# Attention queries: turned once in the projection, stored turned, with the row of maxima placed by a transpose and eight small copies

## Chip, core and metric

The kernel runs on one core of a Trainium2 chip. The metric is the time of one execution in device microseconds (us), the median of several runs. TensorE (PE) multiplies matrices and transposes tiles, VectorE (DVE) and GpSimd (POOL) work on elements, ScalarE (ACT) evaluates functions and copies, SyncE (SP) issues most DMAs. SBUF is the working memory with 128 partitions; PSUM holds what TensorE writes, in eight banks of 128 x 512 float32.

## What is computed

One layer over 2048 latent tokens of width 1024, with 256 context tokens that only supply keys and values:

```python
p_x = modulate(x, norm1_g, sh1, sc1) @ w_in        # k | v | q | gMLP u | gMLP v | two gates
q_x = apply_rope(rmsnorm(q_heads(q_x), q_norm_g), cos, sin) * HEAD_DIM ** -0.5
k_x = apply_rope(rmsnorm(kv_heads(p_x[..., :K_W]), k_norm_g), cos, sin)
s = jnp.einsum('bkgqd,bknd->bkgqn', q, k, preferred_element_type=jnp.float32)
attn = softmax(s) @ v                              # 8 query heads of 64, 2 key heads
x = x + g1 * branch_merge(attn, gmlp, gate_a, gate_b, w_br_attn, w_br_gm, w_out)
x = x + g2 * (jnp.square(jax.nn.relu(modulate(x, norm2_g, sh2, sc2) @ w_ff1)) @ w_ff2)
```

All arrays are float32. The change concerns the queries `q` and the softmax of `s`.

## The kernel before, in words

The kernel has four stages, one after the other: projection (`project`, L994), attention (`attend`, L1109), the merge of the branches with the output projection (`merge`, L1240), and the feed-forward part (`ffn`, L1767). A float32 product is made of float32r products of a rounded "high" half and a remainder, the "low" half.

**Projection.** Tokens come in four blocks of 512 (`TB`), two of them at a time. `pairs_run` (L636) makes the columns up to the gates, `gates` (L965) the gate columns. Beside these products a list `work` of generators is stepped by `tick` (L680), a few operations at a time. One of them is `queries_work` (L755), once for each block of 512 tokens: it loads the raw queries (L760 to L762), normalises each head, rotates it (`rope`, L468; its last VectorE instruction is L483) and stores 128-token rows to the DRAM tensor `q_d[b]` of 512 tokens x 512 columns (L773), in two halves `c` of four heads. `keys_work` (L717) does likewise for the keys, but splits them into halves first (L738, L739), turns them on TensorE by `transposes` (L187; each transpose is at L189) and stores them turned. `mixing` (L802), the gMLP branch, turns its result in the same way (L845 to L855) and stores it by ScalarE's DMA queue (L857).

**Attention.** A unit (class `Unit`, L1989) is two heads of one block of 512 queries: 16 units, four for each block. `attend` goes through a unit's 18 key tiles of 128 keys in three thirds of six (`GROUP`), `gi` = 0, 1, 2. For each key tile, a score step, `first` (L2083) multiplies the keys (high and low halves stacked on 128 partitions) by the high half of the queries, `second` (L2094) adds the high keys times the low half of the queries, and ScalarE takes the exponential of the sum (L2111). The softmax maximum is subtracted inside `second`: partition 0 of the low-query operand holds minus the maximum, one number for each query, and partition 0 of the key operand `KB` holds 1 (the constant `lead`, L203, copied at L1803).

The next units are prepared inside the running one. In the code `nxt` is the unit one later, `far` the one two later, `old` and `older` the ones before. The maxima of `nxt` and `far` come from separate products with high halves alone (`maxima`, L2038: matmuls L2053, VectorE reductions L2059 and L2064). Then, after each third's score steps, come the products with the values of the third before (`values`, L2114; matmuls L2121, row sums on GpSimd L2137 and VectorE L2134), the sums of probabilities (`sums`, L2159), and `join` (L2147). The queries of a unit go this way:

- `load` (L1999), first third, for `far`: one DMA brings 512 tokens x 128 columns into `qt`; GpSimd zeroes a part of `pb` (L2010).
- `cast` (L2012), first third: ScalarE rounds `qt` to the high half, written twice, into `pa` (L2013). `remainder` (L2015), end of the first third: VectorE writes the low half into `pb` (L2016).
- `queries` (L2032), middle third, after the third key tile: eight transposes of `pa` on TensorE (L2026) and two evictions by ScalarE (L2028) give `qa`, the high operand of each head.
- `reference` (L2068), end of the middle third, for `nxt`: VectorE reduces the maxima (L2070) and writes minus the maximum into a column of `pb` (L2071).
- `low_queries` (L2076), after the last third's score steps, for `nxt`: eight transposes of `pb` and two evictions give `qb`, the low operand with the maxima in partition 0.

The first two units are prepared in the projection's closing gates by the function `tail` (L1812).

**What sets the order.** Tile tags name pools of buffers: `h` has 40 (keys, values, query operands), `t4` 8, `t2` 6 (`POOLS`, L55); PSUM has eight banks of tag `b` in attention, four `a` and four `b` in the projection. A scheduler orders the instructions; `order` (L1863) ties it. In attention TensorE and VectorE keep the order of the code, other engines do not; in the projection nearly nothing is fixed. The first writers of the buffers of one tag always keep the order of the code.

## Time and profile before

| what | us |
|---|---|
| median of 3 runs (3070.08 to 3071.9) | 3070.73 |
| the profiled execution's own time | 3072.42 |
| its span, first to last instruction | 3070.6 |
| projection, from the start | about 755 |
| attention, 16 units | 755 to 1436 |
| merge and feed-forward part | 1436 to the end |
| all transposes at L189: TensorE busy in 695 to 755 / 755 to 1436 | 4.25 / 30.02 |

The granted TensorE clock was 0.988 over the span. Views of the profile used below: the page's first part gives busy time by engine; the table of stretches gives busy time of each engine between two moments of the span, with the clock and the DMAs; the timeline lists instructions in order of time, alike ones merged into one line with their count (start, duration, engine, line of the kernel, operation, tiles written <- read, and in brackets the idle time before and what ended it); a line's own view gives shortest, median and longest duration in ns; the waits give who waited for whom, total us, times, and the longest. PEld is TensorE's loading of weights, which overlaps PE. A merged line's duration runs to the end of its last instruction, and TensorE's instructions overlap, so the spacing of starts says more than the durations.

### The profile page before, as it was taken

To read this page: it belongs to the slowest core of one execution; us is meant where nothing else is said; L and a number is where in the kernel's file an instruction comes from. 1 tells how busy PE (TensorE), PEld (TensorE's weight loads), DVE (VectorE), ACT (ScalarE), POOL (GpSimd) and SP (SyncE) were. 2 spreads that over 40 slices of the span, in tenths; PEclk is the share of its full clock that TensorE was granted. 3 is DMA by queue.
4 is the path that set the end of the run, shared out by engine and by line. 5 is a ranking of instruction groups with operands and counts; after the bars stand their busy time and mean duration, and the time that the engine had idled before them with its cause. 6 is when DMAs were issued, how large, how long until landed. Compare 5 with 4: busy or idle time off the path is not lost.

```text
span 3070.6 us, 38002 instructions
## 1 busy us (share of the span) xinstructions
PE 2981.3 (97%) x13501; PEld 2256.5 (73%) x13501; DVE 2070.4 (67%) x3006; ACT 1457.8 (47%) x2350; POOL 656.7 (21%) x488
## 2 busy tenths in 40 slices
PE   6999999989999999999999989999999999999999
PEld 4877788866555555555888878888777888888887
DVE  4876577875887677667655588776576666654555
ACT  5645765653555545545322254444454344444442
POOL 0000000001888888886222200000000000000000
PEclk9999999999999999999999999999999999999999
DMA  8686656644011000004676558888776544448554
GB/s 293 211 268 209 226 191 205 202 152 129 28 36 42 15 5 18 11 8 132 233 214 208 183 171 310 310 302 293 263 227 221 190 152 152 152 152 288 206 206 151
DMA packets 386591, 534.33 MB, mean 174 GB/s; under 512 B 32912, under 2 KB 204096, under 8 KB 386400
## 3 DMA queue, kind: packets, MB, share of 16 engines
q1 hardware_dynamic: 376624, 515.89, 50.4%
q10 hardware_dynamic: 9776, 16.01, 1.4%
q8 instruction: 106, 1.74, 0.2%
q14 instruction: 85, 0.70, 0.1%
HBM read 367.69 MB, written 164.10 MB: 173 GB/s over the span
## 4 chain that ended last, share of the span: by engine, by line
PE 84%; DVE 6%; DMA 5%; ACT 2%; issue 2%; SPq 0%; ACTq 0%; DVEq 0%
PE b L1546 13%; PE b L1545 13%; PE b L1547 13%; PE b L2121 8%; PE b L2088 5%; PE b L2107 4%; PE b L183 4%; PE b L185 4%; PE b L184 4%; PE b L2053 3%; PE a L1545 3%; PE a L1546 3%; PE a L1547 3%; PE b L189 2%; DMA f<-in_w_in 1%
## 5 line engine op out<-in xcount | busy, mean ns | idle before, releaser
L2064 DVE TENSOR_REDUCE ts<-b 128x1 f32<-128x512 f32 x512 | 314.7, 681 | 142.2 <-PE b L2053 142.2
L2137 POOL TENSOR_TENSOR ac<-ac,p 128x512 f32<-128x512 f32 x216 | 300.3, 1423 | 69.4 <-ACT p L2111 68.8
L1661 DVE TENSOR_TENSOR b<-b,b 128x1024 fp32r<-128x1024 f32 x170 | 200.7, 1220 | 128.9 <-ACT b L1660 127.6
L2111 ACT ACTIVATE p<-b 128x512 f32<-128x512 f32 x384 | 199.8, 615 | 167.4 <-PE b L2107 156.2
L1660 ACT CAST b<-b 128x1024 fp32r<-128x1024 f32 x170 | 170.7, 1051 | 225.1 <-PE b L1547 107.9
L1546 PE MATMUL b<-b,b 128*128 128x512 f32 x680 | 266.3, 392 | 5.6 <-DVE b L1661 5.6
L1545 PE MATMUL b<-b,b 128*128 128x512 f32 x680 | 267.1, 393 | 3.3 <-ACT b L1728 1.4
L1547 PE MATMUL b<-b,b 128*128 128x512 f32 x680 | 265.3, 390 | 0.0
L2137 POOL TENSOR_TENSOR ac<-ac,t 128x512 f32<-128x512 f32 x152 | 217.5, 1456 | 0.0
L2088 PE MATMUL b<-h,h 128*128 128x512 f32 x576 | 200.9, 419 | 3.1 <-ACT t L2169 1.7
L2107 PE MATMUL b<-h,h 128*128 128x512 f32 x576 | 180.6, 395 | 0.0
L2121 PE MATMUL b<-p,h 128*64 128x512 f32 x768 | 175.3, 598 | 0.0
L1546 PE MATMUL b<-hb,b 128*128 128x512 f32 x446 | 173.8, 390 | 0.0
L1555 DVE TENSOR_TENSOR f<-f,b 128x512 f32<-128x512 f32 x160 | 109.1, 682 | 82.1 <-issue 48.3
L1545 PE MATMUL b<-hb,b 128*128 128x512 f32 x415 | 161.8, 390 | 0.0
L1547 PE MATMUL b<-hb,b 128*128 128x512 f32 x415 | 161.3, 389 | 0.0
L2010 POOL MEMSET t<- 128x512 f32 x16 | 8.4, 525 | 700.2 <-DMA tb_d<-t 677.9
L1546 PEld LDWEIGHTS b<-b,b 128*128 128x128 f32 x680 | 128.1, 188 | 35.6 <-DVE b L1661 8.9
L1545 PEld LDWEIGHTS b<-b,b 128*128 128x128 f32 x680 | 128.0, 188 | 32.4 <-ACT b L1660 2.5
L2088 PEld LDWEIGHTS b<-h,h 128*128 128x128 f32 x576 | 106.9, 190 | 61.0 <-DVE ts L2064 19.4
L1547 PEld LDWEIGHTS b<-b,b 128*128 128x128 f32 x680 | 128.1, 188 | 26.4
L1558 ACT ACTIVATE f<-f 128x512 f32<-128x512 f32 x96 | 60.5, 630 | 148.8 <-DVE f L1555 148.8
(428 smaller groups left out, 7416.7 us busy)
## 6 DMA issues: line engine op xcount, KB each, us to landing
ao_d<-f SPq DMA_DIRECT2D x224, 256.0 KB
f<-in_w_ff SPq DMA_DIRECT2D x48, 1024.0 KB
b<-ao_d SPq DMA_DIRECT2D x85, 512.0 KB
b<-w2o_d SPq DMA_DIRECT2D x85, 512.0 KB
w2o_d<-f SPq DMA_DIRECT2D x112, 256.0 KB
f<-in_w_in SPq DMA_DIRECT2D x44, 512.0 KB
f<-x_d SPq DMA_DIRECT2D x64, 256.0 KB
hb<-ao_d SPq DMA_DIRECT2D x54, 256.0 KB
```

Of the source, the lines that this page charges most:

```text
L183: mm(ps, sh, mh, start=start, stop=False)
L1545: mm(ps, wh, hh, start=start and k == 0, stop=False, skip_group_check=True)
L1546: mm(ps, wh, hl, start=False, stop=False, skip_group_check=True)
L1547: mm(ps, wl, hh, start=False, stop=k == len(w) - 1, skip_group_check=True)
L1660: nc.scalar.copy(h, f32(l))
L1661: nc.vector.tensor_tensor(out=l, in0=f32(l), in1=f32(h), op=ALU.subtract)
L2064: nc.vector.tensor_reduce(out=self.mx[:, t, h, c : c + 1], in_=ps[h], axis=AX.X, op=ALU.max)
L2088: self.nc.tensor.matmul(self.pts[j][h], k.KA[c][self.kv][:, ks], self.qa[h], start=True, stop=False, skip_group_check=True,)
L2107: self.nc.tensor.matmul(s, k.KB[c][self.kv][:, ks], self.qb[h], start=False, stop=True, skip_group_check=True,)
L2111: self.nc.scalar.activation(pt[h], s, AF.Exp)
L2121: nc.tensor.matmul(self.o[h * HD : (h + 1) * HD, :], k.V[c][:, i, self.kv * HD : (self.kv + 1) * HD], pt[h], start=j == 0, stop=j == NKT - 1,)
L2137: nc.gpsimd.tensor_tensor(out=self.acc[e][:, h], in0=old[:, h], in1=pt[h], op=ALU.add)
```

## The change

`queries_work` turns the rotated queries on TensorE, evicts them by ScalarE and stores them from ScalarE's queue; `q_d[b]` becomes four tensors of 128 columns x 512 tokens, one for each pair of heads, i.e. one for each unit. A unit's `load` brings each head's 64 rows twice, into the upper and the lower 64 partitions (four DMAs of 64 rows). `cast` makes `qa` from that directly, `remainder` makes `qb`; `turned`, `queries` and `low_queries` go, with `pa`, `pb` and the memset. `cast` moves from the first third to the middle one, `remainder` to the end of the last. `reference` only reduces the maxima; `leading`, in the last third after key tile 16, the fifth of its six, transposes the 128 x 8 maxima into an 8 x 128 tile, ScalarE copies it to SBUF, and SyncE issues eight DMAs of 512 bytes each within SBUF that put the pieces into partition 0 of the two `qb`. The sign moves into `lead`, which becomes -1. In `qb`, partitions 1 to 63 now hold low halves; `KB` is zero there.

```diff
--- before.py
+++ after.py
@@ -200,7 +200,7 @@
         nc.vector.memset(self.ones, 1.0)
         self.lead = cp.tile([P, 1], F32, name="lead")
         nc.vector.memset(self.lead, 0.0)
-        nc.vector.memset(self.lead[0:1], 1.0)
+        nc.vector.memset(self.lead[0:1], -1.0)
         self.G1 = cp.tile([P, KC, 2], F32, name="G1")
         self.S1 = cp.tile([P, KC, 2], F32, name="S1")
         self.G2 = cp.tile([P, KC], F32, name="G2")
@@ -215,7 +215,10 @@
         def spill(n, shape):
             return [dp.tile(shape, F32, tag=f"{n}{b}", name=f"{n}_d{b}") for b in range(NB)]
 
-        self.q_d = spill("q", [TB, NH * HD])
+        self.q_d = [
+            [dp.tile([P, TB], F32, tag=f"q{b}_{p}", name=f"q_d{b}_{p}") for p in range(NH // 2)]
+            for b in range(NB)
+        ]
         self.gm_d = spill("gm", [512, TB])
         self.at_d = spill("at", [512, TB])
         self.ta_d = spill("ta", [D, TB])
@@ -770,11 +773,19 @@
             yield
             qo = self.m4([TT, 4, HD])
             self.rope(tabs, raw, qo, self.m4([TT, 4, HD]), 4)
-            nc.sync.dma_start(
-                self.rows(self.q_d[b], slice(c * 256, (c + 1) * 256)),
-                qo.rearrange("p t h d -> p t (h d)"),
-            )
-            yield
+            yield
+            for f in range(2):
+                ps = self.bank([TB])
+                self.transposes(
+                    ps,
+                    [
+                        qo[:, t, 2 * f : 2 * f + 2].rearrange("p h d -> p (h d)")
+                        for t in range(TT)
+                    ],
+                )
+                ot = self.t2([TB])
+                nc.scalar.copy(ot, ps)
+                nc.scalar.dma_start(self.q_d[b][2 * c + f], ot)
 
     def raw_values(self, b, j, c):
         x = self.m4([TT, 4, HD])
@@ -1119,22 +1130,19 @@
                 for j in group:
                     u.first(j)
                     u.second(j)
-                    if j % GROUP == 2 and far:
-                        if gi == 0:
-                            far.load()
-                        elif gi == 1:
-                            far.queries()
+                    if j % GROUP == 2 and far and gi == 0:
+                        far.load()
+                    if j % GROUP == 4 and nxt and gi == 2:
+                        nxt.leading()
                     if not nxt:
                         next(late, None)
                     elif i and j % GROUP == 4:
                         next(mod, None)
-                if gi == 2 and nxt:
-                    nxt.low_queries()
                 if step:
                     step.maxima(3)
                 for f in pend:
                     f()
-                if gi == 0 and far:
+                if gi == 1 and far:
                     far.cast()
                 if gi == 2 and old:
                     old.sums()
@@ -1143,8 +1151,8 @@
                 if gi == 0:
                     if older:
                         older.inverse()
-                    if far:
-                        far.remainder()
+                if gi == 2 and far:
+                    far.remainder()
                 if gi == 1:
                     if nxt:
                         nxt.reference()
@@ -1817,8 +1825,6 @@
                 key_load(0)
                 u.cast()
                 u.remainder()
-            elif (g, p) == (n, 1):
-                u.queries()
             elif (g, p) == (n + 1, 1):
                 low_load(0)
             elif (g, p) == (n, 5):
@@ -1829,8 +1835,6 @@
                     v.cast()
                     v.remainder()
                     value_load((0, 1))
-                if (g, p) == (n, 6):
-                    v.queries()
                 if (g, p) == (n + 1, 6):
                     key_load(1)
                     value_load((2, 3, 4))
@@ -1840,7 +1844,7 @@
                 if (g, p) == (n + 1, 3):
                     u.maxima(len(u.todo))
                     u.reference()
-                    u.low_queries()
+                    u.leading()
                     v.maxima(6)
 
         self.project(tail)
@@ -1998,42 +2002,22 @@
 
     def load(self):
         k, nc = self.k, self.nc
-        self.qt = k.t2([TT, 2, HD])
-        nc.sync.dma_start(
-            self.qt.rearrange("p t h d -> p t (h d)"),
-            k.q_d[self.b].rearrange("(t p) c -> p t c", p=P)[
-                :, :, self.p * P : (self.p + 1) * P
-            ],
-        )
-        self.pa = k.t4([TT, 2, 2, HD], F32R)
-        self.pb = k.t4([TT, 2, P])
-        nc.gpsimd.memset(self.pb[:, :, :, :HD], 0.0)
+        self.raw = [k.t2([TB]) for _ in range(2)]
+        for h, raw in enumerate(self.raw):
+            src = k.q_d[self.b][self.p][h * HD : (h + 1) * HD]
+            for i in range(2):
+                nc.sync.dma_start(raw[i * HD : (i + 1) * HD], src)
 
     def cast(self):
-        self.nc.scalar.copy(self.pa, self.qt.unsqueeze(3).broadcast_to([P, TT, 2, 2, HD]))
+        self.qa = [self.k.h2([TB], F32R) for _ in range(2)]
+        for q, raw in zip(self.qa, self.raw):
+            self.nc.scalar.copy(q, raw)
+        self.mx = self.k.small([TT, 2, NB + 1])
 
     def remainder(self):
-        self.nc.vector.tensor_tensor(
-            out=self.pb[:, :, :, HD:], in0=self.qt, in1=f32(self.pa[:, :, :, 0, :]),
-            op=ALU.subtract,
-        )
-
-    def turned(self, src):
-        k = self.k
-        out = []
-        for h in range(2):
-            ps = k.bank([TB])
-            k.transposes(ps, [src(t, h) for t in range(TT)])
-            q = k.h2([TB], F32R)
-            self.nc.scalar.copy(q, ps)
-            out.append(q)
-        return out
-
-    def queries(self):
-        self.qa = self.turned(
-            lambda t, h: f32(self.pa[:, t, h]).rearrange("p a d -> p (a d)")
-        )
-        self.mx = self.k.small([TT, 2, NB + 1])
+        self.qb = [self.k.h2([TB], F32R) for _ in range(2)]
+        for q, hi, raw in zip(self.qb, self.qa, self.raw):
+            self.nc.vector.tensor_tensor(out=q, in0=raw, in1=f32(hi), op=ALU.subtract)
 
     def maxima(self, n):
         k, nc = self.k, self.nc
@@ -2066,15 +2050,25 @@
                     )
 
     def reference(self):
-        nm = self.k.small([TT, 2])
-        self.nc.vector.tensor_reduce(out=nm, in_=self.mx, axis=AX.X, op=ALU.max)
-        self.nc.vector.tensor_scalar(
-            out=self.pb[:, :, :, 0:1], in0=nm.unsqueeze(3), scalar1=-1.0, scalar2=None,
-            op0=ALU.mult,
-        )
-
-    def low_queries(self):
-        self.qb = self.turned(lambda t, h: self.pb[:, t, h, :])
+        k, nc = self.k, self.nc
+        self.nm = k.small([2, TT])
+        nc.vector.tensor_reduce(
+            out=self.nm.rearrange("p h t -> p t h"), in_=self.mx, axis=AX.X, op=ALU.max
+        )
+
+    def leading(self):
+        k, nc = self.k, self.nc
+        n = 2 * TT
+        ps = k.bank([P])
+        nc.tensor.transpose(ps[:n], self.nm.rearrange("p h t -> p (h t)"), k.ident)
+        row = k.t2([P])
+        nc.scalar.copy(row[:n], ps[:n])
+        for h in range(2):
+            for t in range(TT):
+                nc.sync.dma_start(
+                    f32(self.qb[h])[0:1, t * P : (t + 1) * P],
+                    row[h * TT + t : h * TT + t + 1],
+                )
 
     def keys(self, j):
         c, i = (0, j) if j < CTX // P else ((j - 2) // TT + 1, (j - 2) % TT)
```

## The prediction, made before the result was known

> **What bounds the kernel now.** I read the page first, then the busy time by stretch of the span, then TensorE's timeline inside two attention units.
>
> ```profile
> PE 2981.3 (97%) x13501; PEld 2256.5 (73%) x13501; DVE 2070.4 (67%) x3006; ACT 1457.8 (47%) x2350; POOL 656.7 (21%) x488
> PE 84%; DVE 6%; DMA 5%; ACT 2%; issue 2%; SPq 0%; ACTq 0%; DVEq 0%
> ```
>
> TensorE is busy 97% of the span, and the chain that ended last runs through it for 84%. The next rows (stretch, its length, then busy us of PE, PEld, DVE, ACT, POOL, then clock, DMA share, GB/s) show two stretches of the projection and one attention unit.
>
> ```profile
> 100.00:400.00 300.00, 285.97 (x1359) 236.55 (x1358) 201.03 (x369) 173.62 (x270) 0.00 (x0) 0.99 0.70 230
> 400.00:695.00 295.00, 272.69 (x1281) 231.30 (x1280) 226.18 (x407) 165.71 (x263) 1.05 (x2) 0.96 0.59 185
> 1223.00:1266.00 43.00, 43.00 (x208) 23.73 (x206) 30.16 (x44) 22.23 (x43) 36.22 (x28) 1.00 0.04 13
> ```
>
> In attention TensorE never rests (43.00 of 43.00) at full clock, and no other engine is full. So there each TensorE instruction taken away shortens the unit by its pitch, unless it covered another engine's lag. In the projection TensorE idles 14.0 and 22.3 us: work put there is nearly all paid for. The transposes alone, by stretch:
>
> ```profile
> 695.00:755.00 60.00, 4.25 (x32) 3.60 (x30) 0.98 0.50 158
> 755.00:1436.00 681.00, 30.02 (x232) 27.03 (x232) 0.99 0.08 24
> ```
>
> All 232 of the attention stretch are queries being turned: 14 units x 8 for the high halves, 15 x 8 for the low halves with the maximum; in the closing gates (695 to 755) another 24 of the 32 are. Their 30 us of busy time overlap, so I price them by when the next instruction starts.
>
> **The change, part by part.** Units 13 and 14, TensorE alone. Unit 14 is the last but one: no unit follows its successor, so its middle third turns no queries and is otherwise the same. That is the change's first half, already in the trace.
>
> ```profile
> 1317.34 1.37 PE L2053 MATMUL b<-h,h 64*128 64x512 f32 x6
> 1318.64 3.65 PE L2121 MATMUL b<-p,h 128*64 128x512 f32 x16
> ...
> 1324.84 0.73 PE L2088 MATMUL b<-h,h 128*128 128x512 f32 x2
> ...
> 1331.40 1.03 PE L2053 MATMUL b<-h,h 64*128 64x512 f32 x6
> 1332.42 3.65 PE L2121 MATMUL b<-p,h 128*64 128x512 f32 x16
> ...
> 1338.62 0.89 PE L2088 MATMUL b<-h,h 128*128 128x512 f32 x2
> ...
> 1344.65 1.03 PE L189 MATMUL b<-ident,t 128*128 128x128 f32 x8
> 1345.61 1.39 PE L2053 MATMUL b<-h,h 64*128 64x256 f32 x10
> ...
> 1367.59 0.73 PE L2088 MATMUL b<-h,h 128*128 128x512 f32 x2
> ...
> 1380.40 0.88 PE L2088 MATMUL b<-h,h 128*128 128x512 f32 x2
> ```
>
> A. *High halves no longer turned.* The middle third takes 13.78 us in unit 13 (1324.84 to 1338.62) and 12.81 in unit 14 (1367.59 to 1380.40): 0.97 less. 14 units x 0.97 = **13.6 us**. By a pitch of 0.1 us per transpose alone it would be about 11; that is the lower end.
>
> B. *Low halves no longer turned; a transpose of the maxima five steps into the last third instead.* Eight transposes held TensorE 0.96 us (1344.65 to 1345.61).
>
> ```profile
> L189 PE MATMUL b<-ident,t x296: 270/272/328, 22.9 to 1387.2; 128*128 128x128 f32 x148
> L189 PEldq EVENT_SEMAPHORE  x61: 51/51/2516, 23.3 to 2306.2; - x61
> ```
>
> Against that stand four costs. (1) One new transpose, of 128x8: between 0.12 (0.96 / 8) and 0.27 (one instruction's busy time, nothing overlapped); I take 0.15, near the run of eight. (2) The transposes gave ScalarE time to free banks. At the first third's end, where nothing stands between scores and maxima, the six maxima matmuls take 1.30 us (1317.34 to 1318.64), in the middle third 1.02 (1331.40 to 1332.42): 0.28 of waiting. I take 0.25, bounds 0 and 0.6. (3) ScalarE's copy of the row falls among exponentials: 0.15, bounds 0 and 0.3. (4) The first second-half score matmul waits for eight DMAs: at most 8 x 0.051 = 0.4 of semaphore instructions, if nothing hides them; I take 0.05, since two matmuls run ahead of it. Net 0.96 - 0.60 = 0.36, times 15 = **5.4 us**, with ends of 15 x 0.84 = 12.6 and 15 x -0.61 = -9.
>
> C. *Closing gates.* Three runs of eight, 0.79 (as under D) to 0.96 each, go; one small transpose comes: **2.4 us**, bounds 0 (if VectorE's maxima set the end there) and 2.8.
>
> D. *Projection.* Per 512 tokens 16 transposes (two runs of eight), four ScalarE copies and four stores on ScalarE's queue come in; two SyncE stores go. The branch B code already turns tiles in this way in the same stage:
>
> ```profile
> 286.25 1.04 PE L189 MATMUL b<-ident,m 128*128 128x128 f32 x8
> 287.04 0.48 PE L1545 MATMUL a<-h,f 128*128 128x512 f32 x1
> 287.36 0.39 PE L1546 MATMUL a<-h,f 128*128 128x512 f32 x1
> ```
> ```profile
> PE b L189 <- DVE m L739: 1.3, 1, 1.3
> ```
>
> A run of eight costs 0.79, and 0.09 more in the slower start behind it (0.32 to the next instead of 0.23): 0.88 x 8 = 7.0 us. A wait of TensorE for VectorE's rotation just ahead: keys, turned likewise, cost 1.3 us once in ten runs; I add 1.0, bounds 0 and 8 x 1.3 = 10.4. The copies and stores lie on ScalarE, which is busy 339 of 595 us there. Cost **8.0 us**; ends 0 (all within TensorE's idle time) and 17.
>
> Costed at nothing. On VectorE one subtract becomes two and the small negation goes:
>
> ```profile
> L2016 DVE TENSOR_TENSOR t<-t,t x16: 693/1656/1667, 701.2 to 1328.9; 128x512 f32<-128x512 f32 x16
> L2071 DVE TENSOR_SCALAR t<-ts x16: 174/948/1222, 746.3 to 1384.0; 128x8 f32<-128x8 f32 x16
> ```
>
> The same subtract takes 0.69 us while GpSimd is quiet and 1.66 in attention, so the second costs 1.66, less 0.95: +0.7 us per unit for VectorE, busy 30 of 43. The pair now stands at a unit's end behind the maxima, with six score steps (5.4 us) until VectorE is wanted again; without that cover the pair would cost 3.3 us in each of 14 units, 46 us, and the kernel would be slower. The Trainium skill, page SBUF — State Buffer, section "SBUF: two separate sides", says that a VectorE instruction with two SBUF inputs and a GpSimd instruction that reads SBUF exclude each other for a whole instruction. It speaks against splitting the subtract, and the trace agrees (0.69 against 1.66). On ScalarE one cast of 1024 columns becomes two of 512, four evictions per unit go, and the small copy comes: it is busy 22 of 43 and gets lighter. GpSimd loses its memset. Loads: SyncE issues four for one, long before they are needed.
>
> The row's trip decides the rest. Its steps in unit 6 of before:
>
> ```profile
> 1042.31 0.62 PE L2088 MATMUL b<-h,h 128*128 128x512 f32 x2
> 1042.36 0.20 DVE L2070 TENSOR_REDUCE ts<-ts 128x8 f32<-128x40 f32 x1
> ...
> 1044.12 0.61 PE L2088 MATMUL b<-h,h 128*128 128x512 f32 x2
> 1044.27 2.10 ACT L2111 ACTIVATE t<-b 128x512 f32<-128x512 f32 x4
> ...
> 1055.10 0.63 PE L2107 MATMUL b<-h,h 128*128 128x512 f32 x2
> ```
> ```profile
> 968.72 0.53 ACTq L2172 DMA_DIRECT2D sm_d<-t  x2
> ```
> ```profile
> 970.20 0.32 SPq L2181 DMA_DIRECT2D t<-sm_d  x1
> ```
>
> The maxima are reduced at 1042.56, 1.5 us before the transpose's place (1044.12). It ends by 1044.4; ScalarE has two or four exponentials ahead (1045.3 or 1046.4), the copy perhaps 0.3. Then SyncE issues eight one after the other at about 0.32 each (the last row), 2.6 us, ending by 1048.2 to 1049.3. Landing: the load at 970.20 waited for a 2 KB store whose second part was issued by 969.25, so 0.95 us. The row is in place by 1049.2 to 1050.3. Its reader, at 1055.10 now, comes about 0.6 earlier: 4.2 us to spare. Before the trip TensorE does not wait; behind it stand all of the next unit's exponentials and sums. The Trainium skill, page DMA: Bandwidth & Descriptors, section "Anatomy of one DMA — SWDGE (gpsimd) path", puts a DMA's fixed cost at about 2.0 us, on another issuing path; by it the spare would be an estimated 3 us, and the sum the same.
>
> Sum: 13.6 + 5.4 + 2.4 - 8.0 = 13.4 us less. The profiled execution took 3072.42 (span 3070.6); that would become 3059.0. The median of the runs, 3070.73, is 1.7 lower, so I forecast **3057 us**.
>
> **The rivals.**
> 1. *The projection takes more back.* Nothing pins its order; the new runs of transposes use the banks and small tiles that the evictions of the main product also pass through, and VectorE is busy 226 of 295 us. For: VectorE's rotations are its slowest steps there. Against: the trace holds one such wait of 1.3 us. With 10 us instead of 1: about 3066.
> 2. *The row comes late, and the kernel is slower.* SyncE serves in order; a load that waits for a buffer would hold the eight copies up, and every unit's second half-score with them. The point: with more than 4.2 us added, TensorE stops, 15 times over. Each us beyond costs 15; 13.4 / 15 = 0.9 beyond makes it even. With 2 us beyond, 30 - 13.4: about 3087. For: the stop would hit a unit's very start, where nothing else is ready. Against: the spare, and SyncE nearly empty in most units.
> 3. *ScalarE's two casts and copy land among the exponentials*, where it is already the slower (2.10 us for two steps' four, against 1.81 for TensorE's two steps, 1042.31 to 1044.12). If a third of their 1.5 us is not made up, 0.5 x 14 = 7: about 3064. Against: in those steps ScalarE has no gap to put them in.
> 4. *Idle time in the projection hides its transposes*: D near 0 to 2: about 3050, within the forecast's range.
>
> **How the numbers follow.** Forecast with rival 4 (3048 to 3064): 0.64. Rival 3 (around 3064): 0.10, half on either side of the line. Rival 1 (3064 to 3071): 0.15. Rival 2: 0.11. The range 3048 to 3068 takes in the forecast, rival 3 and half of rival 1, about 0.8; its low end is about all favourable ends but half of B's, its high end the projection's upper cost. 0.2% (6.1 us) is about what a measurement of this kernel can tell from no change. So faster than 3064.6: 0.64 + 0.05 = 0.69; within: 0.05 + 0.15 = 0.20; slower: 0.11.
>
> **What would show it.** A: middle thirds of 12.8 us. B: last thirds about 0.4 shorter, with TensorE not idle ahead of the unit's first second-half score; if it idles there for a DMA, rival 2. C: the first score earlier by 2 us beyond the projection's shift. D: attention starting some 6 us later; more, with TensorE waiting for VectorE or ScalarE at the new transposes, is rival 1. A wrong forecast would come from SyncE's order or from the projection being laid out anew.

## The result and the profile after

| | before | after |
|---|---|---|
| median of 5 runs, us | 3071.0 (3070.08 to 3075.13) | 3055.59 (3055.49 to 3060.24) |
| profiled execution, us | 3072.42 | 3055.49 |
| span, us | 3070.6 | 3053.4 |
| first score matmul of attention at | 754.74 | 755.88 |
| first matmul of the merge at (idle just before it) | 1437.49 (1.75) | 1417.56 (6.99) |
| from there to the end of the span | 1633.1 | 1635.8 |

After over before is 0.9946, with a 95% interval of 0.9933 to 0.9959: 15.4 us faster by the medians, 17.2 by the two spans. The spans divide into stages: the first score comes 1.1 us later; between first score and first merge matmul 682.75 us became 661.68, and without the idle time at its end 681.00 became 654.69, so attention itself lost 26.3; the idle time ahead of the merge grew by 5.2; the rest is 2.7 longer. 1.1 - 26.3 + 5.2 + 2.7 = -17.3.

The first lines of the page of the changed kernel, engines with busy time and share. TensorE is still the engine that bounds it, with 21 us less to do.

```profile
PE 2960.3 (97%) x13325; PEld 2232.3 (73%) x13325; DVE 2093.8 (69%) x3006; ACT 1438.3 (47%) x2334; POOL 659.8 (22%) x472
```

TensorE's timeline of the changed kernel, from the start of a middle third over the last third behind it (start, duration, line, operation). The transposes and evictions are gone; L2063 is the one new transpose, of the maxima.

```profile
1017.54 0.74 PE L2082 MATMUL b<-h,h 128*128 128x512 f32 x2
...
1030.34 0.88 PE L2082 MATMUL b<-h,h 128*128 128x512 f32 x2
...
1035.48 0.27 PE L2063 MATMUL b<-ident,ts 128*8 128x128 f32 x1
1035.50 0.70 PE L2082 MATMUL b<-h,h 128*128 128x512 f32 x2
1036.05 0.63 PE L2101 MATMUL b<-h,h 128*128 128x512 f32 x2
1036.61 1.23 PE L2037 MATMUL b<-h,h 64*128 64x256 f32 x10
1037.76 3.65 PE L2115 MATMUL b<-p,h 128*64 128x512 f32 x16
...
1044.81 0.89 PE L2082 MATMUL b<-h,h 128*128 128x512 f32 x2
1045.54 0.63 PE L2101 MATMUL b<-h,h 128*128 128x512 f32 x2
```

The last third before, in unit 13, from behind its transposes and maxima:

```profile
1346.94 3.65 PE L2121 MATMUL b<-p,h 128*64 128x512 f32 x16
...
1353.99 0.89 PE L2088 MATMUL b<-h,h 128*128 128x512 f32 x2
```

Four readings. The middle third that ends at 1030.34 began at 1017.54: 12.80 us, as forecast. The last third takes 14.47 us (1030.34 to 1044.81); before it took 15.37 (1338.62 to 1353.99), so it lost 0.90, where 0.36 was forecast. The maxima, which stood behind the old transposes, take 1.15 us (1036.61 to 1037.76); before they took 1.33 (1345.61 to 1346.94), so without the transposes they got shorter, not longer. The new transpose and the pair of score matmuls behind it take 0.57 us (1035.48 to 1036.05) where a pair takes 0.46, so it costs 0.11; TensorE isn't idle ahead of 1045.54, the first second-half score.

The row's trip in the same unit, on ScalarE and SyncE (the second fence is the eight copies' own line, in ns):

```profile
1036.55 0.24 ACT L2065 COPY t<-b 8x128 f32<-8x128 f32 x1
1036.82 4.95 SPq L2068 DMA_DIRECT2D h<-t  x8
```
```profile
L2068 SPq DMA_DIRECT2D h<-t x128: 497/587/602, 750.3 to 1368.4; - x128
```

The eight copies take SyncE 4.95 us, 0.587 each in the median, nearly twice the 0.32 of the forecast. SyncE is done at 1041.77, so it was not late here, but the spare is smaller.

The merge's start, from SyncE's, ScalarE's and TensorE's timelines of the changed kernel:

```profile
1411.25 0.35 ACTq L2139 DMA_DIRECT2D at_d<-t  x1
```
```profile
1413.33 0.39 SPq L1229 DMA_DIRECT2D bw<-in_w_br_attn  x1
1413.83 0.44 SPq L1229 DMA_DIRECT2D bw<-in_w_br_gm  x1
```
```profile
1416.88 1.14 ACT L150 CAST bw<-bw 128x512 fp32r<-128x512 f32 x2 [5.66 <-DMA bw<-in_w_br_gm]
```
```profile
1417.56 0.79 PE L183 MATMUL b<-in,bw 128*128 128x512 f32 x1 [6.99 <-ACT bw L150]
```
```profile
SPq L1229 <- DMA at_d<-t: 28.6, 1, 28.6
```

The merge's first weight load (L1229) goes out only after the last unit's output has been stored (L2139; the last line shows SyncE waiting 28.6 us for that store); the cast and then TensorE wait behind it. This loss stood nowhere in the prediction. The reading that merge_fix below tests: the merge's pools lie where attention's were, and the first `bw` tile covers the `t2` buffer that held the last unit's output. Before, the first load waited for the store of a row of sums instead, and went out at 1403.9. The change takes five `t2` buffers a unit where there were three, and so the last output moved to another of the six.

### The profile page after: what moved, and what is told of

Read it like the earlier page. It is cut to its first block, busy times and chain, and to the rows that moved or that the text cites. A ratio compares the mean times of both kernels' runs of the same rounds, so it can differ in the third digit from the quotient of the medians.

```text
span 3053.4 us, 37883 instructions
## 1 busy us (share of the span) xinstructions
PE 2960.3 (97%) x13325; PEld 2232.3 (73%) x13325; DVE 2093.8 (69%) x3006; ACT 1438.3 (47%) x2334; POOL 659.8 (22%) x472
## 5 line engine op out<-in xcount | busy, mean ns | idle before, releaser
L2131 POOL TENSOR_TENSOR ac<-p,p 128x512 f32<-128x512 f32 x32 | 47.9, 1518 | 770.3 <-ACT p L2105 770.3
L1553 PE MATMUL a<-f,h 128*128 128x384 f32 (+1 forms) x320 | 119.0, 376 | 12.1 <-ACT a L650 4.9
```

What stands on the lines that cost most here:

```text
L1553: mm(ps, wh, hh, start=start and k == 0, stop=False, skip_group_check=True)
L2131: nc.gpsimd.tensor_tensor(out=self.acc[e][:, h], in0=old[:, h], in1=pt[h], op=ALU.add)
```

## The experiments

Theory, from the two traces: attention gained more than forecast because the old transposes cost not only TensorE's pitch but also two banks and ScalarE's evictions; the projection's price is unclear; the merge lost some 5 us to a reused buffer. Rivals: the forecast's own terms (B 0.36 a unit, D 8 us), and for the merge that something else is late there. The profiled executions give the stages (first score, first merge matmul with its idle time, span, all us):

| kernel | first score | first merge matmul | idle before | span |
|---|---|---|---|---|
| no_turn | 752.9 | 1409.8 | 1.8 | 3047.4 |
| before_turns | 768.5 | 1451.2 | 1.8 | 3083.5 |
| before_turns_dry | 768.1 | 1450.9 | 1.8 | 3081.6 |
| merge_fix | 759.2 | 1416.4 | 1.8 | 3052.2 |
| eight_back | 756.3 | 1429.1 | 7.1 | 3065.7 |
| eight_back_evict | 759.6 | 1437.3 | 7.4 | 3073.9 |
| row_late | 758.1 | 1503.7 | 7.0 | 3137.6 |
| rem_early | 759.0 | 1438.7 | 1.8 | 3075.1 |
| row_late_two | 759.9 | 1431.4 | 7.2 | 3066.5 |
| stores_back | 769.8 | 1428.4 | 1.8 | 3062.4 |
| gates_back | 761.2 | 1421.0 | 1.8 | 3058.1 |
| merge_fix_two | 758.8 | 1417.3 | 1.8 | 3058.1 |

Kernels with the same projection and closing gates as the changed one begin attention between 755.9 and 759.9: one profile gives that stage to some 4 us, the stages after it much closer. Medians below stand beside the ratio to the kernel before on the same chip, whose own median was 3071.8 for the first eight and 3075.0 for the last four.

**B: eight_back and eight_back_evict.** The old eight transposes go back to their old place, without and with evictions; results unread. This is eight_back_evict; eight_back has one bank for both heads, `[k.bank([TB])] * 2`, and no copy.

```diff
+                if gi == 2 and nxt:
+                    nxt.again()
                 if step:
                     step.maxima(3)
...
+    def again(self):
+        k = self.k
+        ps = [k.bank([TB]) for _ in range(2)]
+        for h in range(2):
+            k.transposes(
+                ps[h], [f32(self.qa[h])[:, t * P : (t + 1) * P] for t in range(TT)]
+            )
+            self.nc.scalar.copy(ps[h], ps[h])
```

> The changed kernel with eight transposes put back at the old place, ahead of the last third's maxima, into one bank that nothing reads: no eviction, one bank. Theory TensorE (the gain of B is the transposes' pitch alone): 15 x 0.8 to 0.96 = 12 to 14.4 us, 3068 to 3070, and the variant with evictions is the same. Theory of the prediction (they gave ScalarE time to free banks): 0.96 - 0.25 = 0.7 x 15 = 10.7, 3066, or less. Theory banks and ScalarE (the old transposes cost more by their two banks and 1.16 us of evictions): about 10 here, and 3 to 5 us more in the variant with evictions.

> As eight_back (3068.7 us; 11.1 us more than the changed kernel between the first score matmul and the first merge matmul, 0.74 per unit), but the eight transposes go into two banks, and ScalarE copies both banks (onto themselves): the old last third's load in full, except that nothing waits for the result. Theory TensorE alone: no more than eight_back, 3069. Theory banks and ScalarE: the last third is 0.90 or more longer than in the changed kernel (14.47 us), 15 x 0.16 to 0.3 = 2.4 to 4.5 us above eight_back, 3071 to 3073. The prediction's term (2), that the evictions' time came free for ScalarE's lag, expects the last third to be shorter than eight_back's: under 3068.

Measured: 3068.74 (0.9987, 0.9978 to 0.9997) and 3075.17 (1.0008, 0.9998 to 1.0017). Attention without the idle time at its end is 11.0 and 15.6 us longer than in the changed kernel: 0.73 and 1.04 for each of 15 units. TensorE's timelines at the place, first eight_back:

```profile
1041.56 1.04 PE L189 MATMUL b<-ident,h 128*128 128x128 f32 x8
1042.52 0.97 PE L2039 MATMUL b<-h,h 64*128 64x256 f32 x10
1043.42 3.65 PE L2125 MATMUL b<-p,h 128*64 128x512 f32 x16
```

and eight_back_evict:

```profile
1046.80 1.04 PE L189 MATMUL b<-ident,h 128*128 128x128 f32 x8
1047.77 1.30 PE L2039 MATMUL b<-h,h 64*128 64x256 f32 x10
1049.00 3.65 PE L2126 MATMUL b<-p,h 128*64 128x512 f32 x16
```

Both put 0.96 to 0.97 us of transposes in. In eight_back the maxima behind them take 0.90 us (1042.52 to 1043.42) instead of 1.15 in the changed kernel: 0.25 comes back, the size of the forecast's term (2). With the evictions they take 1.23, and nothing comes back; in the kernel before they took 1.33. So transposes alone do shorten what stands behind them, as term (2) had it, and their own evictions and banks use that up. The banks and ScalarE's time were put back together; which of the two counts isn't separated.

**D: no_turn.** The changed kernel's projection without the turning.

```diff
-                ps = self.bank([TB])
-                self.transposes(
...
-                ot = self.t2([TB])
-                nc.scalar.copy(ot, ps)
-                nc.scalar.dma_start(self.q_d[b][2 * c + f], ot)
+                nc.scalar.dma_start(
+                    self.q_d[b][2 * c + f].rearrange("p (t c) -> p t c", c=P),
+                    qo[:, :, 2 * f : 2 * f + 2].rearrange("p t h d -> p t (h d)"),
+                )
```

> The changed kernel without the turning in the projection: the 64 transposes and 16 evictions go, the rotated queries are stored unturned by ScalarE's queue; the queries that attention reads are therefore not the turned ones. In this kernel the memory under the merge's first weight tile is another's than the last output's, so it is compared with merge_fix and by the time of the first score matmul (755.88 us in the changed kernel). Prediction's term D (8 us): first score 7 to 8 us earlier, 748, and the whole 8 below merge_fix. Reading of the two traces (the first score came only 1.1 us later although the closing gates lost 2.4 us of transposes): 3.5 us, first score at 752.4, 3.5 below merge_fix. Rival 4 (hidden in idle time): 0 to 2 us.

Measured: 3053.1 (0.9930, 0.9918 to 0.9943), against merge_fix's 3052.17 (0.9931): no difference. The first score came 3.0 us earlier than in the changed kernel, 6.3 earlier than in merge_fix. So 0 to 6 us; the 8 of the forecast is too much here, and the run doesn't part the other two. Nor is the turning all that differs: TensorE waits 5.49 us for the last load of the mixing in no_turn and 0.34 in merge_fix, so what the run gives is the turning less that wait.

**D from the other side: before_turns and before_turns_dry.** The kernel before, with the same 64 transposes and 16 evictions added; the dry one leaves out the last line, the store.

```diff
             yield
+            for f in range(2):
+                ps = self.bank([TB])
+                self.transposes(
...
+                ot = self.t2([TB])
+                nc.scalar.copy(ot, ps)
+                nc.scalar.dma_start(self.x_d[b][2 * c + f], ot)
```

> The kernel before, with the 64 transposes, 16 evictions and 16 stores of the changed projection added, into rows of DRAM that nothing reads. Prediction's term D without the stores that go: 8 us, 3079. Reading of the traces: 3.5 us, 3074.5, with the first score at 758.3 instead of 754.74. Hidden in idle time: 3071 to 3073.

> As before_turns (the kernel before with 64 transposes and 16 evictions added in the projection, 3084.9 us against 3071.8), but without the 16 extra stores (4 MB): the turned tiles are dropped. If the turning itself costs the 13 us: 3083 to 3085. If the extra stores' traffic and ScalarE's issuing cost most of it: 3075 to 3079, which leaves the turning 4 to 7 us. Hidden in idle time: 3072.

Measured: 3084.9 (1.0040, 1.0028 to 1.0053) and 3084.6 (1.0043, 1.0030 to 1.0055). Both are 13 us slower, so the extra 4 MB of stores from ScalarE's queue cost nothing and the turning 13 us, where the forecast's D has 8. The row of the stretch up to the first score, before and then before_turns (length, busy us of PE, PEld, DVE, ACT, POOL, clock, DMA share, GB/s):

```profile
0.00:754.74 754.74, 693.77 (x3237) 562.70 (x3237) 516.26 (x960) 424.40 (x688) 2.28 (x9) 0.97 0.65 212
```
```profile
0.00:768.50 768.50, 705.91 (x3302) 572.89 (x3302) 519.88 (x961) 433.63 (x704) 2.28 (x9) 0.96 0.66 214
```

TensorE is busy 12.1 us longer and idle 1.6 longer (60.97 to 62.59): on the whole the idle time hid nothing. Where the 13 us arise can be read from the first of the mixing's products, with half of the turning done; it starts at 279.32 before and at 293.29 in before_turns, 14 us later. The cause stands at the second of the four runs of eight there:

```profile
204.11 1.94 PE L189 MATMUL b<-ident,m 128*128 128x128 f32 x8 [3.61 <-DVE m L487]
208.40 0.80 PE L1561 MATMUL a<-f,h 128*128 128x512 f32 x1 [2.35 <-ACT a L651]
```
```profile
208.00:212.00 4.00, 3.60 (x9) 2.83 (x10) 1.26 (x5) 3.96 (x9) 0.00 (x0) 0.50 1.02 366
```

TensorE waits 3.61 us for VectorE's rotation and 2.35 for ScalarE right behind, and the clock is granted at 0.50 between 205 and 212. With 0.68 of waiting at the run before, that is 6.6 us of idle time; four runs at the forecast's 0.88 are 3.5, and the half clock took, by an estimate from these rows, some 4 of the rest. The changed kernel has the same wait (3.61 at 200.34), and its first mixing product is 7.4 us late (286.69). The second half of the turning adds next to nothing in before_turns (14.0 late at 293, 13.8 at the first score). So it isn't the pitch that the forecast had too small but the wait for VectorE, priced at 1.0.

But if the turning costs 13 and the changed kernel pays some 3, something in the change gives back about as much as the forecast's whole gain.

**stores_back.** Ahead of the closing gates, the one other thing that the change does in the projection is to drop SyncE's stores of the unturned queries. They go back, unread, into merge_fix.

```diff
+            nc.sync.dma_start(
+                self.rows(self.x_d[b], slice(c * 256, (c + 1) * 256)),
+                qo.rearrange("p t h d -> p t (h d)"),
+            )
             yield
```

> merge_fix (3052.2 us) with one part of the change undone: SyncE also stores the unturned rotated queries, as before, to rows that nothing reads. In the kernel before, the same 64 transposes cost 13 us (before_turns), in the changed kernel taking them out gave 0 to 5 (no_turn). Theory stores: the eight SyncE stores that the change removes held up other loads of the projection in order; putting them back costs 4 to 8 us, 3056 to 3060, with the last mixing product later than merge_fix's 699.55 by as much and waiting for its DMA again (5 us as in before_turns; 0.3 in merge_fix). Rival (stores are free, as the prediction had it): within 2 us of 3052.

Measured: 3061.91 (0.9963, 0.9948 to 0.9977), 6.5 us over merge_fix by each one's distance from the kernel before, 9.8 by the ratios; the first score came 10.6 later. The stores are not free. The last of the mixing's products comes 9.3 us later, after a wait for its load, first stores_back, then merge_fix:

```profile
708.83 0.55 PE L183 MATMUL b<-m,m 128*128 128x256 f32 x1 [5.64 <-DMA m<-ws_d]
```
```profile
699.55 0.38 PE L183 MATMUL b<-m,m 128*128 128x256 f32 x1 [0.34 <-DMA m<-ws_d]
```

That load on SyncE's timeline, in the same order, and what SyncE waited for ahead of it in merge_fix:

```profile
681.30 22.93 SPq L1942 DMA_DIRECT2D tb_d<-t  x4
704.33 0.38 SPq L845 DMA_DIRECT2D m<-ws_d  x1
```
```profile
679.16 8.75 SPq L1937 DMA_DIRECT2D tb_d<-t  x2
695.47 0.32 SPq L840 DMA_DIRECT2D m<-ws_d  x1
```
```profile
SPq L840 <- DVE m L154: 7.5, 1, 7.5
```

With the stores the scheduler puts four gate stores ahead of the load, each waiting for ScalarE's tanh; without them only two stand there. That order alone doesn't explain the delay, though. In merge_fix the load goes out when an instruction of the mixing on VectorE (L154) is done, at 695.45, and in stores_back that instruction is done only at 702.61. If the load needs that instruction there too, as the same code suggests, the gate stores held it back by 1.7 us at most. The mixing itself was 7.2 us late, and 5.0 of the delay stand already at the fifth of its eight products (616.69 against 611.65). The kernel before waits there too (5.78 at 692.07), and its load goes out (688.23) as L154 ends (688.21), not held by the gate stores. So it is shown that the stores cost 6.5 to 10.6 us, in a stage that the scheduler lays out anew with them; by which mechanism isn't. Nor is the wait decisive by itself, since no_turn had 5.49 us of it and still began attention earliest.

**C: gates_back.** The closing gates' three runs of eight transposes with their evictions go back into merge_fix.

```diff
+            elif (g, p) == (n, 1):
+                u.again()
...
+                if (g, p) == (n, 6):
+                    v.again()
...
+                    u.again()
                     u.leading()
```

> merge_fix (3052.2 us) with the closing gates' 24 transposes and 6 evictions put back at their old places, reading turned queries, results unread. Prediction's term C: 2.4 us, 3054.6. Theory of the evictions (as in the last thirds, 1.07 us for eight transposes with their two evictions): 3.2 us, 3055.4. By the span from the last mixing product to the first score (59.8 us in the changed kernel, 64.9 in before_turns, 62.7 in before): 2.8 to 5.1, 3055 to 3057.

Measured: 3059.5 (0.9946, 0.9935 to 0.9958), 4.1 over merge_fix by the distances. From the last mixing product (698.27; merge_fix 699.55) to the first score are 62.9 us, against 59.65: 3.3. That is 1.1 for each run of eight with evictions, as in the last thirds.

**The merge's start: merge_fix.**

```diff
-        oc = k.t2([TB])
+        oc = k.t4([TB]) if self.last else k.t2([TB])
```

> The changed kernel with one edit: the last unit's output is copied into a tile of another group, so that the merge's first weight load doesn't overlay it and needn't wait for its store. If that wait is what the merge lost (load issued at 1413.33, cast at 1416.88, first matmul at 1417.56 after 6.99 us of idle time): the loads go out before 1390, the first matmul comes at 1411.5 to 1412.5, and the time is 5 to 6 us lower, near 3050. Rival: the merge's start waits for something else that is as late (input rows, gate rows), and the time stays within 1 us of 3055.6.

Measured: 3052.17 (0.9931, 0.9918 to 0.9943), 4.2 below the changed kernel by the distances from the kernel before; the two intervals overlap, so the stages have to carry it:

```profile
L1229 SPq DMA_DIRECT2D bw<-in_w_br_attn x32: 379/384/1266, 1388.9 to 1712.0; - x32
```
```profile
1416.39 0.50 PE L183 MATMUL b<-in,bw 128*128 128x512 f32 x1 [1.80 <-ACT bw L150]
```

The loads go out at 1388.9, and the idle time falls from 6.99 to 1.80, which is the 1.75 of the kernel before. Between first score and first merge matmul 661.7 became 657.2. The buffer was the cause of the wait.

**The remainder's cover: rem_early.**

```diff
+                if gi == 2 and far:
+                    far.remainder()
                 if gi == 2 and old:
                     old.sums()
                 if step:
                     step.maxima(3)
...
-                if gi == 2 and far:
-                    far.remainder()
```

> The changed kernel with the two subtracts put ahead of the last third's second three maxima steps, so that their reductions queue behind 3.4 us of VectorE work on banks that the next unit's scores need. If the cover is what makes the subtracts free: up to 3.3 us in each of 14 units, some 20 to 46 us more, 3076 to 3102, TensorE waiting for VectorE's reductions at the maxima or the next scores. Rival (the eight banks and VectorE's spare time take it up): within 2 us of 3056.

Measured: 3076.52 (1.0012, 1.0003 to 1.0021). The first merge load doesn't wait here either, so it stands against merge_fix: attention is 22.5 us longer. VectorE's timeline with TensorE's at a unit's end, and a later row of TensorE's:

```profile
1058.68 3.45 DVE L2020 TENSOR_TENSOR h<-t,h 128x512 fp32r<-128x512 f32 x2
...
1062.05 3.67 DVE L2048 TENSOR_REDUCE ts<-b 128x1 f32<-128x512 f32 x6
```
```profile
1062.78 0.50 PE L2082 MATMUL b<-h,h 128*128 128x512 f32 x1 [1.00 <-DVE ts L2048]
```

The reductions start 3.4 us late, and the next unit's second score matmul waits about 1 us a unit for a bank (1.7 in early units). In two early units it waits 2.8 and 2.9 us; there the trace names a load of queries that lands at the same time, but TensorE goes on 0.73 us after the first late reduction starts (843.80 and 844.53), just as here (1062.05 and 1062.78). The cover that the prediction named is real. In the changed kernel the same pair, 3.40 us, runs from 1048.05 to 1051.45 beside the score steps, and TensorE waits for nothing.

**The row's trip: row_late and row_late_two.** `leading` moves behind the last third's value matmuls; then also two copies in place of eight.

```diff
-                    if j % GROUP == 4 and nxt and gi == 2:
-                        nxt.leading()
...
+                if gi == 2 and nxt:
+                    nxt.leading()
                 if gi == 2 and old:
                     old.sums()
```
```diff
-            for t in range(TT):
-                nc.sync.dma_start(
-                    f32(self.qb[h])[0:1, t * P : (t + 1) * P],
-                    row[h * TT + t : h * TT + t + 1],
-                )
+            nc.sync.dma_start(f32(self.qb[h])[0:1], row[h * TT : (h + 1) * TT])
```

> The changed kernel with the transpose of the maxima, its copy and the eight row copies issued behind the last third's value matmuls, some 6 us later than now, three maxima steps ahead of the next unit's first score. With the issue time read in the changed kernel's trace (8 x 0.587 to 0.62 us, 4.9 in all, and 0.95 landing) the row is in place at about 1048 by unit 6's clock, 2 to 2.5 us after its reader's place (1045.54): 15 x 2 to 2.5 = 30 to 38 us more, 3086 to 3094, with TensorE waiting for a DMA at the first second-half score. With the prediction's 0.32 us an issue (2.6 in all) it is in place at about 1045.5: no loss, 3056.

> As row_late (3141.6 us), but two row copies, one per head with four source rows, instead of eight. In row_late the eight took SyncE 4.95 us (1029.39 to 1034.34) and TensorE idled 1.22 and 2.23 us for them, then ran at clock 0.50 for some 5 us. Theory issue: with two copies SyncE is done by 1030.6, the row is in place by 1031.4 to 1031.8, the reader's place is 1031.8; no or 0.3 us of waiting a unit, no drop of the clock: 3052 to 3061, though the row still leaves 6 us late. Theory of the place alone (whatever leaves so late is late, by the copy and the landing): at least half of the 86 us stays, over 3098.

Measured: row_late 3141.57 (1.0225, 1.0209 to 1.0240), 86 us more than the changed kernel, over twice the expected loss. The timeline, then the stretches behind it (columns as above):

```profile
1028.80 0.27 PE L2063 MATMUL b<-ident,ts 128*8 128x128 f32 x1
...
1029.39 4.95 SPq L2068 DMA_DIRECT2D h<-t  x8
...
1033.02 0.47 PE L2101 MATMUL b<-h,h 128*128 128x512 f32 x1 [1.22 <-DMA h<-t]
...
1035.72 0.77 PE L2101 MATMUL b<-h,h 128*128 128x512 f32 x1 [2.23 <-DMA h<-t]
```
```profile
1036.28:1041.40 5.12, 5.12 (x13) 3.97 (x12) 0.00 (x0) 2.95 (x6) 2.53 (x2) 0.50 0.30 84
1041.40:1043.40 2.00, 2.00 (x11) 1.36 (x9) 0.00 (x0) 1.98 (x5) 1.44 (x2) 1.00 0.00 0
```

Each unit waits twice, 3.45 us together here; over attention the waits sum to 55.2 us. The other 30 fit the clock: after the waits it was granted at 0.50 for 5.12 us here, then 1.00 again, and over the span at 0.975, against 0.986 in the changed kernel. From the last issue's end (1034.34) to its reader are 1.38 us, where 0.95 was forecast for a landing. By that, the changed kernel's row lands at 1043.15, 2.4 us ahead of its reader at 1045.54; the forecast had 4.2.

row_late_two, with the row leaving just as late, took 3068.66 (0.9979, 0.9969 to 0.9990): 10 us more than the changed kernel instead of 86, so it was the eight issues. It came out above the expected 3061, mostly for one unit:

```profile
1375.59 3.68 SPq L1199 DMA_DIRECT2D raw<-at_d  x3
1380.62 0.51 SPq L1203 DMA_DIRECT2D gx<-rs_d  x1
1381.22 1.25 SPq L2067 DMA_DIRECT2D h<-t  x2
```
```profile
1383.32 1.22 PE L2097 MATMUL b<-h,h 128*128 128x512 f32 x2 [4.75 <-DMA h<-t]
```

There the merge's input loads stand ahead of the row on SyncE; of 5.9 us that TensorE waits for rows in attention, 4.75 are this one, and behind it the clock is at 0.50 until about 1388. That is the forecast's rival 2, in one unit of fifteen, and only once the spare has been used up.

**merge_fix_two.** Both edits, from merge_fix and row_late_two, in the changed kernel.

> merge_fix (3052.2 us) with two row copies a unit instead of eight. The row's trip has 2.7 us to spare in the changed kernel, so shortening it by 3.5 us should change nothing by itself: 3050 to 3054. If SyncE's 4.9 us a unit delayed other transfers that matter: up to 1 us for some units, 3045 to 3050.

Measured: 3051.36 (0.9928, 0.9915 to 0.9941), not told apart from merge_fix. The shorter trip only adds spare. Either kernel is 20 to 24 us faster than the one before, and 4 to 8 faster than the change, by each one's distance from the kernel before.

## Why the prediction was right, and where two errors cancelled

3057 was forecast and 3055.6 measured, inside 3048 to 3068 and with a gain of 15.4 against 13.4. The mechanism held in attention: TensorE, which is full there, was relieved of the transposes, and the row came in time. That the total lies within 2 us is luck: B gave 8 us more than forecast, and a loss that stood nowhere in the prediction (5.2 at the merge's start) and a longer last stretch (2.7) took as much back. Inside D two errors cancelled as well. The terms:

- **A, right.** Middle third 12.80 as forecast, 0.98 x 14 = 13.7 us.
- **B, too small: 5.4 forecast, 13.5 read from the last thirds, 11.0 to 15.6 by putting it back.** The 13.5 is above the term's own best end, 12.6. The failing step is (2). Its 0.25 us is real for transposes alone, but ScalarE's evictions and the two banks that went with them were left out, and they take the 0.25 back: the maxima behind got 0.18 shorter (1.33 to 1.15), where 0.25 longer was forecast. (1), (3) and (4), 0.35 in all, came to 0.24: the score steps of the third take 6.27 us (1030.34 to 1036.61) against 6.03 (1338.62 to 1344.65), 0.11 of it the new transpose. 0.96 + 0.18 - 0.24 = 0.90.
- **C, a little small: 2.4 forecast, 3.3 measured,** above its upper bound of 2.8, by the same omission.
- **D, too large, and made of two errors: 8.0 forecast, some 3 to 6 by the stages, none by the times.** The turning alone costs 13: the wait for VectorE's rotation, priced at 1.0, is 3.61 us at one run, with more idle time and a halved clock behind it. The SyncE stores that go, costed at nothing, give 6.5 to 10.6 back. The failing steps are that wait and "two SyncE stores go" without a price; why the stores cost so much stays open. The prediction did name the projection "laid out anew" as what could make it wrong.
- **Costed at nothing.** The subtracts' cover is real (22.5 us when it is taken away). The row's trip had the right answer with a wrong issue time (0.32 for 0.587) and landing (0.95 for 1.38): spare 2.4, not 4.2.
- **Not foreseen: the merge's start, 5.2 us more idle time.** merge_fix takes it back. The prediction followed `t2` only inside attention, not to the next stage that reuses its memory.

Rival 1 didn't decide the total, but its mechanism is there: the waits of 6.6 us at the first runs, with the half clock behind them, are the larger part of the 14 us in before_turns. Rival 2 didn't occur; row_late shows its price, 5.7 us a unit. Rival 3 left no trace: the middle third with the casts takes 12.80 us, unit 14's of before without them 12.81. Rival 4, idle time as cover, is refuted for the kernel before as a whole.

The measured terms sum to 13.7 + 13.5 + 3.3 - (0 to 6) - 5.2 = 19 to 25 us, over the 15.4 to 17.2 seen. 2.7 of the difference is the longer stretch behind the first merge matmul, which no run explains; by the tables it is 1630.7 to 1633.1 us in the three kernels with the old attention and 1633.9 to 1640.8 in the eleven with the new one, so part of it can be the scatter of single profiles. Up to 4 is how far the projection differs from run to run. The rest stays open, as does D within its 0 to 6.

## What to carry to other kernels

Price a transpose with its eviction and its bank, not by TensorE's pitch alone, above all where ScalarE frees the banks that the next matmuls need, and with the wait for the engine that makes its input. Where a scheduler lays out a stage, a transfer that goes can have a price too: put it back by itself to learn it, and don't take the first wait in sight for the reason. When a change alters how many buffers a rotation takes, follow the last ones into the next stage, whose first loads may lie on them.

## What the runs showed of the hardware

**A wait of about 3 us can cost more than its length.** The granted clock was 0.50 for 5.12 us after row_late's 3.45 us of waiting in two pieces, for about 5.5 us after the changed kernel's 6.99 at the merge, and 0.50 just after a wait of 2.87 in rem_early. The rows of the stretches, first the changed kernel, then rem_early, then merge_fix behind its 1.80:

```profile
1417.50:1423.00 5.50, 5.44 (x13) 4.24 (x14) 2.49 (x4) 1.66 (x4) 0.00 (x0) 0.50 1.01 338
```
```profile
844.50:846.50 2.00, 1.97 (x5) 1.58 (x6) 2.00 (x4) 0.65 (x2) 1.73 (x2) 0.50 0.24 73
```
```profile
1416.40:1421.00 4.60, 4.60 (x19) 3.44 (x20) 3.16 (x5) 1.50 (x3) 0.00 (x0) 1.00 0.67 218
```

After 1.80 us it stayed at 1.00. The Trainium skill, page TensorE: Matmul & The Clock Gate, section "Part 1: The HAM clock gate (the "warmup" mystery)", says that an idle window of about 3.4 us drops TensorE to half its clock and about 3.4 us of sustained work restores it. The halving agrees; here a wait of 2.87 us sufficed, and the half clock lasted longer than that, 5.5 us in the changed kernel's row.

**A small copy within SBUF is not cheap to issue.** The eight 512-byte copies cost SyncE 0.587 us each in the median, and the last was 1.38 us from the end of its issue to its reader.
